# Sparse attention in a two-layer trunk: a third PSUM bank for scores and transposes, gate multiplications on GpSimd, first scores issued between the tiles of memory attention

## The chip, the cores and the metric

The kernel runs on one core of one Trainium2 chip. The metric is the device time of one execution in microseconds (us); the time of a kernel is the median of its runs. Everything is fp32 data. The engines are called as in the profile: PE (TensorE, matrix multiplications and transposes), DVE (VectorE), ACT (ScalarE), POOL (GpSimd), SP (SyncE, which issues most DMA transfers here).

## What is computed

The reference is a trunk of two layers over a sequence of 512 tokens of width 1024. Layer 0 is gated linear attention; layer 1, with which this case deals, is sparse attention with 12 heads of width 64 in 4 groups. Both layers add an attention to a memory of 256 tokens (4 heads), an output projection, and a feed-forward block with a short convolution. The part around the change, cut down:

```python
def nsa_mixer(q, gates, shared, rel_bias):
    kc, vc, ks, vs, kw, vw = shared              # compressed, selected and window keys and values, 4 groups
    ...
        s_c = jnp.einsum('bgrqd,bgkd->bgrqk', qb, kc) + common_bias(d_c)    # 31 compressed keys
        p_c = masked_softmax(s_c, d_c >= 0)
        o_c = jnp.einsum('bgrqk,bgkd->bgrqd', p_c, vc)
        ...
        s_s = jnp.einsum('bgrqd,bgqkd->bgrqk', qb, k_sel) + group_bias(d_s) # selected blocks
        p_s = masked_softmax(s_s, (d_s >= 0)[:, :, None])
        ...
        s_w = jnp.einsum('bgrqd,bgkd->bgrqk', qb, kwb) + common_bias(d_w)   # window
        p_w = masked_softmax(s_w, mask_w)
        ...
        o = gb[..., 0:1] * o_c + gb[..., 1:2] * o_s + gb[..., 2:3] * o_w    # one gate a head and branch
```

16 blocks may be selected and there are only 8, and the window is as long as the sequence, so the selected branch and the window branch are both plain causal attentions over all keys, with keys and values of their own. The gates are sigmoids, one for each token, head and branch.

## The kernel before

**Products.** Most large matrix products are made of three: weights and activations are split into a high and a low part (`wget` for weights: a load of 512 KB, where a gain belongs to it a multiplication on POOL, line 232; the high part `wh` on ACT, line 235; the low part `wl = wraw - wh` on DVE, line 236. `split_to` for activations: high on ACT, line 249, low on DVE, line 250), and high x high, high x low and low x high are accumulated in one bank.

**PSUM.** The eight banks are four pairs, with the tags `acc`, `sc`, `pt` and `po`; asking for a tag gives the next free one of its pair.

**The stage of the change** is the loop over six pairs of heads, `a` = 0 to 5 (heads a and a+6, called hh 0 and 1), in `nsa_layer`. Each pair is done in two steps `s`: first query tiles 0 and 3 (128 and 512 keys), then tiles 1 and 2 (256 and 384 keys), so 12 steps. Generators make the pieces:

- `project(a)`: queries of one pair, 24 matmuls of 512 columns in one `acc` bank, evicted by DVE (line 961, `qf`).
- `queries(a)`: copies of the queries by DMA (`dup`), a strip of bias values from DRAM (line 974), and the split in `Qh` (ACT, line 249) and `Ql` (DVE, line 250).
- `compressed(a)`, in three parts. First: the 31 compressed keys in 8 small products, with `kcT`; both evictions with the bias (DVE, line 1037); minimum and subtraction (DVE, 1040 and 1041; all scores are negated, hence a minimum); exponential (ACT, 1042). Second: mask of the first tile (`cmask`, DVE, 1044), sum and reciprocal (DVE, 1046 to 1048), times the gate (DVE, 1050), and `Pc` times that (DVE, 1051, 128x256). Third: four transposes of `Pc` into a `pt` bank (PE, 947), copied out by ACT (1056).
- `scores(s)`, in six parts, three for each head: a pair of matmuls (K with Qh, K with Ql) into an `sc` bank. For the short tile of a step both branches go into one bank; for the long tile each branch has a bank, so there are the short one, then branch 0, then branch 1. Each is evicted by DVE (line 1078: adds the bias, writes `P` to SBUF and keeps the minimum `smn`) and goes through the exponential on ACT (1080), which also sums (`ssm`). After a head's last part: reciprocal of the sums (DVE, 1082), times the gates (DVE, 1085, 128x4), and then POOL multiplies both `P` tiles of that head by them (1088).
- `weights_t(s)`, in six parts: PE transposes `P` (line 947) into a `pt` bank, and ACT or DVE copies it out (1105, `PT`).
- `values(s)`: PE multiplies `PT` by V and `PcT` by the compressed values (`vcz`) into a `po` bank, one bank for a pair of heads over its two steps.

**What sets the order.** On PE the order of this stage is written by hand: `pe()` chains every matmul and transpose (`mm`, `tr`, lines 946 and 947) to the one before it. In each step there are six rounds; a round issues one part of `scores(s+1)`, one part of `weights_t(s)`, two matmuls of `project(a+2)` (while there is one), and, at fixed rounds, parts of `compressed`, `queries` and `values(s-1)`. The projections of the pairs 0 and 1 come earlier, between the tiles of the memory attention (`mem_att` calls `upto`, which runs the generator `others`). On DVE, ACT, POOL and SP a scheduler sets the order from the order of the program and its own costs; each engine then works in that order.

Of the kernel before, what the change touches and what calls it, by code (L numbers as in the profile page):

```python
# [14 lines left out]
AF = mybir.ActivationFunctionType  # L15
ALU = mybir.AluOpType
# [155 lines left out]
class Trunk:  # L172
# [638 lines left out]
    def nsa_layer(self):  # L811
        nc, I, tc = self.nc, self.I, self.tc
        rc, rb = self.rms_finish(S, "")
        GKV, GMIX = 6, 1
        with ExitStack() as outer:
            pool = outer.enter_context(tc.tile_pool(name="nsa", bufs=1))
            mo = [tuple(self.t(pool, [128, S], f"mo{m}{c}", FR) for c in "hl") for m in range(2)]
            K = [self.t(pool, [128, 2, S], f"K{g}", FR) for g in range(4)]
# [9 lines left out]
            with tc.tile_pool(name="nsap", bufs=2) as pp:  # L828
                T = [self.t(pp, [128, 4, S], f"T{j}", bufs=1) for j in range(2)]
                for j in range(2):  # L830
                    for m in range(2):
# [4 lines left out]
                        for hh in range(2):  # L836
                            g = 2 * m + hh
# [142 lines left out]

            run = lambda g, n=1: [next(g, None) for _ in range(n)]

            with ExitStack() as ms:
                mk = ms.enter_context(tc.tile_pool(name="memk1", bufs=1, side="right"))
                mK, mV = self.mem_kv(1, mk)
                mp = ms.enter_context(tc.tile_pool(name="mema1", bufs=1, side="right"))
# [8 lines left out]
                def others():  # L995

                    gen = project(0)
                    for _ in range(8):
                        yield run(gen, 3)
                    q = queries(0)  # L1000
                    run(q)
                    for i, _ in enumerate(values()):
                        if i == 16:
                            run(q, 3)
                        yield
                    gen = project(1)
                    for _ in range(8):
                        yield run(gen, 3)
# [8 lines left out]
            with tc.tile_pool(name="nsac", bufs=2) as cp:  # L1017
# [4 lines left out]
                def compressed(a):  # L1022
# [3 lines left out]
                    pcs = [self.ps("sc") for _ in range(2)]  # L1026
# [17 lines left out]
                    nc.vector.tensor_tensor(out=Pv[:, 6:8, :], in0=Pv[:, 6:8, :], in1=cmask.unsqueeze(1).to_broadcast([128, 2, 32]), op=ALU.mult)  # L1044
# [5 lines left out]
                    nc.vector.tensor_tensor(out=f.rearrange("p (n b) -> p n b", n=4), in0=f.rearrange("p (n b) -> p n b", n=4), in1=g, op=ALU.mult)  # L1050
                    nc.vector.tensor_tensor(out=Pv, in0=Pv, in1=f.unsqueeze(2).to_broadcast([128, 8, 32]), op=ALU.mult)
# [6 lines left out]

                def scores(s):


                    a, qts = steps[s]
                    for hh in range(2):
                        g = (a + 6 * hh) // 3
                        Q, st = Qs[a][hh], strips[a][hh]
                        f = self.t(self.small, [128, 2, 2], "ssm", bufs=6)
                        for j, qt in enumerate(qts):
                            n = 128 * (qt + 1)
                            ts = slice(128 * qt, 128 * qt + 128)
                            P = Ps[a, qt, hh] = self.t(cp, [128, 2, n], f"P{qt}")  # L1070
                            bias = bass.AP(tensor=st.tensor, offset=st.offset + 383 + n, ap=[st.ap[0], [-1, n]])
                            mn = self.t(self.small, [128, 2], "smn", bufs=6)
                            for brs in ((0, 1),) if qt < 2 else ((0,), (1,)):
                                sc = self.ps("sc")
                                for i in range(2):
                                    mm(sc[:, :n * len(brs)], Q[i][:, ts], K[g][:, brs[0]:brs[-1] + 1, :n], start=i == 0, stop=i == 1)
                                for br in brs:
                                    nc.vector.tensor_tensor_reduce(out=P[:, br, :n], in0=sc[:, n * (br - brs[0]):n * (br - brs[0]) + n], in1=bias, scale=1.0, scalar=3e38,
                                                                   op0=ALU.add, op1=ALU.min, accum_out=mn[:, br:br + 1])
                                    nc.scalar.activation(P[:, br, :n], P[:, br, :n], AF.Exp, scale=-1.0, bias=mn[:, br:br + 1], accum_out=f[:, j, br:br + 1])  # L1080
                                if qt == qts[1] and brs[-1]:
                                    nc.vector.reciprocal(f, f)
                                    gt = bass.AP(tensor=gates.tensor, offset=gates.offset + 36 * qts[0] + 18 * hh + 3 * a + 1,
                                                 ap=[gates.ap[0], [36 * (qts[1] - qts[0]), 2], [1, 2]])
                                    nc.vector.tensor_tensor(out=f, in0=f, in1=gt, op=ALU.mult)  # L1085
                                    for i, t in enumerate(qts):
                                        P = Ps[a, t, hh]
                                        nc.gpsimd.tensor_tensor(out=P, in0=P, in1=f[:, i, :].unsqueeze(2).to_broadcast([128, 2, 128 * t + 128]), op=ALU.mult)  # L1088
                                yield

                def weights_t(s):

                    a, qts = steps[s]
                    for hh in range(2):
                        for qt in qts:
# [3 lines left out]
                            for brs in ((0, 1),) if qt < 2 else ((0,), (1,)):  # L1099
                                pt = self.ps("pt")  # L1100
# [34 lines left out]
                first = scores(0)  # L1135
                for i in range(6):
                    run(first)
                    if i in (1, 3):
                        run(c)
                for s, (a, qts) in enumerate(steps):  # L1140
# [7 lines left out]
                    for i in range(6):  # L1148
# [12 lines left out]
                        if a and qts[0] == 0 and i in (0, 1):  # L1161
                            run(c)
# [32 lines left out]
```

## Time and profile before

| what | value |
|---|---|
| runs | 1338.71, 1340.07 and 1347.0 us, median 1340.07 us |
| the profiled execution | 1337.29 us on the device, its span on the core 1335.5 us |
| PE busy | 1299.7 us, 97% of the span |
| DVE, ACT, POOL busy | 831.7, 591.1 and 119.8 us |
| mean granted TensorE clock | 0.993 of full |
| the stage of the change | from about 769 us (end of memory attention) to about 924 us (output projection) |

A row of the timeline reads: start and duration in us, engine, line, operation, tile written <- tiles read, shape, and count where alike neighbours were put together; in square brackets how long the engine had been idle before, and what ended that. A row of the windows has a stretch of time, its length, busy time and count of each engine, the granted clock of PE, and the share and rate of DMA. In the views of groups, mean durations are in ns.

### The profile page before, as it was taken

How to read it: one execution, taken by the hardware profiler on the slowest of the kernel's cores; microseconds unless marked ns; L12 is line 12 of the kernel's file. 1: busy time of each engine (PE TensorE's matmuls, PEld its weight loads, DVE VectorE, ACT ScalarE, POOL GpSimd, SP SyncE). 2: the span in 40 equal slices, each digit the busy share in tenths (PEclk: the TensorE clock that was granted, in tenths of full speed). 3: DMA queues.
4: the chain of work that ended last, by engine and by line, in shares of the span. 5: the costliest groups of instructions: out<-in, count | busy, mean ns of one | idle time of the engine just before them, and what ended most of it. 6: DMA issues, size and time to landing. Idle time of an engine off the chain costs nothing. (4 is left out here: it accounts for less than half of the span.)

```text
span 1335.5 us, 18101 instructions
## 1 busy us (share of the span) xinstructions
PE 1299.7 (97%) x6934; PEld 1058.8 (79%) x6934; DVE 831.7 (62%) x1372; ACT 591.1 (44%) x1063; POOL 119.8 (9%) x100
## 2 busy tenths in 40 slices
PE   9999998999999999999999988999999999999997
PEld 6887776878888888888788766778878888888886
DVE  7656777567777775334556677675577777773232
ACT  7446554444444443223224565665444444443221
POOL 1000000000000000002114253342000000000000
PEclk9999998999999999999999989999999999999999
DMA  7342110323333333333567223211333333333321
GB/s 249 103 128 78 32 48 17 114 82 100 100 99 95 95 95 95 98 104 111 139 179 227 78 72 93 73 47 32 96 94 96 95 95 95 96 101 102 96 79 63
DMA packets 43002, 129.96 MB, mean 97 GB/s; under 512 B 5719, under 2 KB 9975, under 8 KB 42916
## 3 DMA queue, kind: packets, MB, share of 16 engines
q1 hardware_dynamic: 41504, 126.96, 32.0%
q10 hardware_dynamic: 1412, 1.85, 0.5%
q8 instruction: 55, 0.90, 0.3%
q14 instruction: 31, 0.25, 0.1%
HBM read 116.16 MB, written 2.15 MB: 89 GB/s over the span
## 5 line engine op out<-in xcount | busy, mean ns | idle before, releaser
L236 DVE TENSOR_TENSOR wl<-wraw,wh 128x1024 fp32r<-128x1024 f32 x196 | 245.6, 1253 | 165.3 <-ACT wh L235 163.1
L235 ACT ACTIVATE wh<-wraw 128x1024 fp32r<-128x1024 f32 x196 | 207.5, 1060 | 275.5 <-PE acc L741 92.5
L267 PE MATMUL acc<-xh,wh 128*128 128x512 f32 x800 | 312.9, 391 | 0.0
L267 PE MATMUL acc<-xl,wh 128*128 128x512 f32 x800 | 312.0, 390 | 0.0
L267 PE MATMUL acc<-xh,wl 128*128 128x512 f32 x800 | 310.5, 390 | 0.0
L267 PEld LDWEIGHTS acc<-xh,wh 128*128 128x128 f32 x800 | 150.2, 188 | 32.8 <-issue 1.3
L267 PEld LDWEIGHTS acc<-xl,wh 128*128 128x128 f32 x800 | 150.2, 188 | 31.6 <-issue 0.2
L267 PEld LDWEIGHTS acc<-xh,wl 128*128 128x128 f32 x800 | 150.2, 188 | 31.5 <-issue 0.5
L741 PE MATMUL acc<-ah,wl 128*128 128x512 f32 x352 | 137.0, 389 | 0.0
L741 PE MATMUL acc<-ah,wh 128*128 128x512 f32 x352 | 137.0, 389 | 0.0
L741 PE MATMUL acc<-al,wh 128*128 128x512 f32 x352 | 137.0, 389 | 0.0
L722 DVE TENSOR_TENSOR u<-acc,rb 128x512 f32<-128x512 f32 x88 | 60.6, 688 | 71.2 <-PE acc L267 69.8
L249 ACT ACTIVATE ah<-hc 128x512 fp32r<-128x512 f32 x44 | 27.8, 632 | 116.0 <-DVE hc L729 116.0
L232 POOL TENSOR_TENSOR wraw<-wraw,vec 128x1024 f32<-128x1024 f32 x20 | 38.7, 1942 | 434.6 <-DMA wraw<-in_wp 410.7
L741 PEld LDWEIGHTS acc<-ah,wl 128*128 128x128 f32 x352 | 66.1, 188 | 13.8
L741 PEld LDWEIGHTS acc<-ah,wh 128*128 128x128 f32 x352 | 66.1, 188 | 13.8
L741 PEld LDWEIGHTS acc<-al,wh 128*128 128x128 f32 x352 | 66.1, 188 | 13.5
L724 ACT ACTIVATE hc<-u,vec 128x512 f32<-128x512 f32 x88 | 71.1, 807 | 2.4 <-DVE u L722 1.6
L1088 POOL TENSOR_TENSOR P<-P,ssm 128x256 f32<-128x256 f32 (+3 forms) x48 | 62.4, 1321 | 79.0 <-DVE ssm L1085 43.2
L725 DVE SCALAR_TENSOR_TENSOR hc<-u,vec,hc 128x511 f32<-128x511 f32 x88 | 65.6, 745 | 5.2 <-ACT hc L724 5.2
L726 DVE SCALAR_TENSOR_TENSOR hc<-u,vec,hc 128x510 f32<-128x510 f32 x88 | 66.0, 750 | 3.1
L728 ACT ACTIVATE hc<-hc 128x512 f32<-128x512 f32 x44 | 27.8, 633 | 83.1 <-DVE hc L726 83.1
(334 smaller groups left out, 2050.8 us busy)
## 6 DMA issues: line engine op xcount, KB each, us to landing
wraw<-in_wp SPq DMA_DIRECT2D x200, 512.0 KB, 3.7
strip<-vecd SPq DMA_DIRECT2D x12, 448.0 KB, 3.9
qd<-qf SPq DMA_DIRECT2D x40, 128.0 KB, 2.4
mt<-in_memT SPq DMA_DIRECT2D x16, 128.0 KB, 2.9
kd<-kf SPq DMA_DIRECT2D x16, 128.0 KB, 2.4
out<-wraw SPq DMA_DIRECT2D x3, 512.0 KB, 3.3
h<-in_xT SPq DMA_DIRECT2D x4, 256.0 KB, 6.7
h<-in_xT ACTq DMA_DIRECT2D x4, 256.0 KB, 6.9
```

The source lines that it names most:

```text
L232: nc.gpsimd.tensor_tensor(out=v, in0=v, in1=g, op=ALU.mult)
L235: nc.scalar.activation(wh, raw, AF.Copy)
L236: nc.vector.tensor_tensor(out=wl, in0=raw, in1=wh.bitcast(F32), op=ALU.subtract)
L249: nc.scalar.activation(hi, src, AF.Copy)
L267: self.nc.tensor.matmul(ps[:M, :N], u[:, M * k:M * k + M], x[k][i][:, :N], start=n == 0, stop=n == 23)
L722: nc.vector.tensor_tensor(out=u, in0=ps, in1=rb, op=ALU.mult)
L724: nc.scalar.activation(c, u, AF.Identity, scale=tap(2), bias=tap(3))
L725: nc.vector.scalar_tensor_tensor(out=c[:, 1:], in0=u[:, :S - 1], scalar=tap(1), in1=c[:, 1:], op0=ALU.mult, op1=ALU.add)
L726: nc.vector.scalar_tensor_tensor(out=c[:, 2:], in0=u[:, :S - 2], scalar=tap(0), in1=c[:, 2:], op0=ALU.mult, op1=ALU.add)
L728: nc.scalar.activation(hc[0], hc[0], AF.Silu)
L741: nc.tensor.matmul(ps, a[:, o], x, start=n == 0, stop=n == 3 * NJ - 1)
L1088: nc.gpsimd.tensor_tensor(out=P, in0=P, in1=f[:, i, :].unsqueeze(2).to_broadcast([128, 2, 128 * t + 128]), op=ALU.mult)
```

## The change

Four things are changed, all in `nsa_layer`.

1. **A third bank.** Scores of branch 1 of a long tile go to a `po` bank instead of `sc`; the compressed scores use one `po` and one `sc` bank instead of two `sc`. In the steps 0 to 7 (while there are projections, the last of which frees its `acc` bank in step 7) the transposes of branch 1 of a long tile go to an `acc` bank instead of `pt`.
2. **Gates on GpSimd.** Four of the lines move from DVE to POOL: the mask of `Pc`, the gates on `cf`, `Pc` times `cf`, and the gates on `ssm`. That is 6 + 6 + 6 + 24 = 42 instructions; the count of PE's instructions stays as it was.
3. **The first scores earlier.** `scores(0)` is no longer made after the memory attention, but its six parts go between the groups of three matmuls of `project(1)`, which lie between tiles of the memory attention. The `P` tiles therefore come from a pool (`nsaw`) opened before, two of each as before.
4. **The order of compressed.** Its second part comes in round 0 of the first step of a pair, as before, and its third (the transposes of `Pc`) in round 5 instead of round 1, now for pair 0 too.

The diff, cut (what stands in `scores` and is not shown is the same as before):

```diff
+            def scores(s):
                 a, qts = steps[s]
...
-                            P = Ps[a, qt, hh] = self.t(cp, [128, 2, n], f"P{qt}")
+                        P = Ps[a, qt, hh] = self.t(wp, [128, 2, n], f"P{qt}", bufs=2)
...
-                                sc = self.ps("sc")
+                            sc = self.ps("po" if brs == (1,) else "sc")
...
-                                    nc.vector.tensor_tensor(out=f, in0=f, in1=gt, op=ALU.mult)
+                                nc.gpsimd.tensor_tensor(out=f, in0=f, in1=gt, op=ALU.mult)
...
                 mK, mV = self.mem_kv(1, mk)
+                wp = outer.enter_context(tc.tile_pool(name="nsaw", bufs=1))
...
-                    gen = project(1)
-                    for _ in range(8):
+                    gen, first = project(1), scores(0)
+                    for i in range(8):
+                        if i in (0, 1, 2, 4, 5, 6):
+                            run(first)
                         yield run(gen, 3)
...
-                    pcs = [self.ps("sc") for _ in range(2)]
+                    pcs = [self.ps(tag) for tag in ("po", "sc")]
...
-                    nc.vector.tensor_tensor(out=Pv[:, 6:8, :], in0=Pv[:, 6:8, :], in1=cmask...
+                    nc.gpsimd.tensor_tensor(out=Pv[:, 6:8, :], in0=Pv[:, 6:8, :], in1=cmask...
...
-                    nc.vector.tensor_tensor(out=f.rearrange(...), in0=f.rearrange(...), in1=g, op=ALU.mult)
-                    nc.vector.tensor_tensor(out=Pv, in0=Pv, in1=f.unsqueeze(2)..., op=ALU.mult)
+                    nc.gpsimd.tensor_tensor(out=f.rearrange(...), in0=f.rearrange(...), in1=g, op=ALU.mult)
+                    nc.gpsimd.tensor_tensor(out=Pv, in0=Pv, in1=f.unsqueeze(2)..., op=ALU.mult)
...
-                                pt = self.ps("pt")
+                                pt = self.ps("acc" if brs == (1,) and s < 8 else "pt")
...
-                first = scores(0)
-                for i in range(6):
-                    run(first)
-                    if i in (1, 3):
-                        run(c)
...
-                        if a and qts[0] == 0 and i in (0, 1):
+                        if qts[0] == 0 and i in (0, 5):
                             run(c)
```

How this moves instructions, at three places. (The numbers in the names are those of tiles; the same number is the same tile.)

**First place, PE around the end of the memory attention.** `L946` is `mm`, `L947` is `tr`; `acc<-xh,wh` is the projection of pair 1, `K,Qh` and `K,Ql` are scores of pair 0, `kcT,qf` compressed scores. Before, after the memory attention and the last two of the compressed products:

```order
L946 MATMUL sc_6431<-kcT_5193,qf_6025 128x31
L946 MATMUL sc_6432<-kcT_5193,qf_6025 128x31
L946 MATMUL sc_6452<-K_952_5188,Qh_1173_6215 128x256
L946 MATMUL sc_6452<-K_952_5188,Ql_1174_6216 128x256
L946 MATMUL sc_6461<-K_952_5188,Qh_1173_6215 128x512
L946 MATMUL sc_6461<-K_952_5188,Ql_1174_6216 128x512
L946 MATMUL sc_6473<-K_952_5188,Qh_1173_6215 128x512
L946 MATMUL sc_6473<-K_952_5188,Ql_1174_6216 128x512
L946 MATMUL sc_6485<-K_954_5190,Qh_1176_6221 128x256
L946 MATMUL sc_6485<-K_954_5190,Ql_1177_6222 128x256
L947 MATMUL pt_6492<-ident_101,Pc_6441 64x128 x4
L946 MATMUL sc_6500<-K_954_5190,Qh_1176_6221 128x512
```

Now, within the projection of pair 1, ahead of the last products of the memory attention:

```order
L946 MATMUL sc_6430<-K_954_5190,Qh_1176_6224 128x256
L946 MATMUL sc_6430<-K_954_5190,Ql_1177_6225 128x256
L946 MATMUL acc_6390<-xh_4889,wh_6386 128x512
L946 MATMUL acc_6390<-xh_4889,wl_6387 128x512
L946 MATMUL acc_6390<-xl_4890,wh_6386 128x512
L946 MATMUL sc_6442<-K_954_5190,Qh_1176_6224 128x512
L946 MATMUL sc_6442<-K_954_5190,Ql_1177_6225 128x512
L946 MATMUL acc_6390<-xh_4982,wh_6386 128x512
L946 MATMUL acc_6390<-xh_4982,wl_6387 128x512
L946 MATMUL acc_6390<-xl_4983,wh_6386 128x512
L946 MATMUL po_6450<-K_954_5190,Qh_1176_6224 128x512
L946 MATMUL po_6450<-K_954_5190,Ql_1177_6225 128x512
```

The six score pairs of step 0 stood alone behind the compressed products, with the transposes of `Pc` among them; now three projection matmuls stand between any two of them, and the compressed products come behind them all.

**Second place, PE in the second half of step 0.** `ident,P` are transposes of weights. Before:

```order
L946 MATMUL sc_6605<-K_954_5190,Qh_1176_6221 128x384
L946 MATMUL sc_6605<-K_954_5190,Ql_1177_6222 128x384
L947 MATMUL pt_6611<-ident_101,P_1237_6498 128x128 x4
L946 MATMUL acc_6544<-xl_4710,wh_6540 128x512
L946 MATMUL acc_6544<-xh_4796,wh_6540 128x512
L946 MATMUL sc_6619<-K_954_5190,Qh_1176_6221 128x384
L946 MATMUL sc_6619<-K_954_5190,Ql_1177_6222 128x384
L947 MATMUL pt_6628<-ident_101,P_1237_6498 128x128 x4
L946 MATMUL acc_6544<-xh_4796,wl_6541 128x512
L946 MATMUL acc_6544<-xl_4797,wh_6540 128x512
L946 MATMUL sc_6639<-K_952_5188,Qh_1267_6597 128x256
```

Now:

```order
L946 MATMUL sc_6602<-K_954_5190,Qh_1176_6224 128x384
L946 MATMUL sc_6602<-K_954_5190,Ql_1177_6225 128x384
L947 MATMUL pt_6608<-ident_101,P_1224_6440 128x128 x4
L946 MATMUL acc_6534<-xl_4710,wh_6530 128x512
L946 MATMUL acc_6534<-xh_4796,wh_6530 128x512
L946 MATMUL po_6616<-K_954_5190,Qh_1176_6224 128x384
L946 MATMUL po_6616<-K_954_5190,Ql_1177_6225 128x384
L947 MATMUL acc_6625<-ident_101,P_1224_6440 128x128 x4
L946 MATMUL acc_6534<-xh_4796,wl_6531 128x512
L946 MATMUL acc_6534<-xl_4797,wh_6530 128x512
L947 MATMUL pt_6633<-ident_101,Pc_6496 64x128 x4
L946 MATMUL sc_6642<-K_952_5188,Qh_1266_6594 128x256
```

The second branch's scores and transposes have the tags `po` and `acc`, and the transposes of `Pc` now close the step, ahead of the first scores of step 2.

**Third place, DVE and POOL where the compressed weights of a pair meet its scores.** DVE before, for pair 1, from the last score eviction of a step to the first of the next (`ISA` is line 1078's eviction, `ssm` the sums, `cf` the factors of the compressed part):

```order
L1044 TENSOR_TENSOR Pc_6726<-Pc_6726,cmask_5199 128x64
L961 SCALAR_TENSOR_TENSOR qf_6765<-acc_6544,rb_5175 128x512
L1046 TENSOR_REDUCE cf_6819<-Pc_6726 128x8
L1082 RECIPROCAL ssm_6697<-ssm_6697 128x4
L1047 TENSOR_SCALAR cf_6819<-cf_6819 128x8
L1085 TENSOR_TENSOR ssm_6697<-ssm_6697,gates_5198 128x4
L1048 RECIPROCAL cf_6819<-cf_6819 128x8
L1050 TENSOR_TENSOR cf_6819<-cf_6819,gates_5198 128x8
L1051 TENSOR_TENSOR Pc_6726<-Pc_6726,cf_6819 128x256
L236 TENSOR_TENSOR wl_7430<-wraw_7426,wh_7429 128x1024
L1078 ISA P_1315_6794,smn_6795<-sc_6796,strip_6520 128x256
```

DVE now:

```order
L1081 TENSOR_REDUCE cf_6822<-Pc_6729 128x8
L961 SCALAR_TENSOR_TENSOR qf_6768<-acc_6534,rb_5175 128x512
L1004 RECIPROCAL ssm_6700<-ssm_6700 128x4
L1082 TENSOR_SCALAR cf_6822<-cf_6822 128x8
L1083 RECIPROCAL cf_6822<-cf_6822 128x8
L236 TENSOR_TENSOR wl_7433<-wraw_7429,wh_7432 128x1024
L1000 ISA P_1315_6797,smn_6798<-sc_6799,strip_6510 128x256
```

POOL now, for pair 0 in step 0 (before, there stood only the multiplications of `P` and the memsets):

```order
L1068 MEMSET Pc_6496 128x8
L1079 TENSOR_TENSOR Pc_6496<-Pc_6496,cmask_5199 128x64
L1007 TENSOR_TENSOR ssm_6512<-ssm_6512,gates_5198 128x4
L1010 TENSOR_TENSOR P_1243_6513<-P_1243_6513,ssm_6512 128x512
L1085 TENSOR_TENSOR cf_6538<-cf_6538,gates_5198 128x8
L1010 TENSOR_TENSOR P_1253_6544<-P_1253_6544,ssm_6512 128x768
L1086 TENSOR_TENSOR Pc_6496<-Pc_6496,cf_6538 128x256
```

The four multiplications have left DVE's queue, where `wl` now follows the reciprocal; in POOL's queue `Pc` times `cf` stands behind both multiplications of `P` of a head.

More of the change, by code (lines that the diff above doesn't have):

```diff
@@ L979, in queries @@
                     yield
+            def scores(s):
+                a, qts = steps[s]
+                for hh in range(2):
+                    g = (a + 6 * hh) // 3
+                    Q, st = Qs[a][hh], strips[a][hh]
+                    f = self.t(self.small, [128, 2, 2], "ssm", bufs=6)
+                    for j, qt in enumerate(qts):
+                        n = 128 * (qt + 1)
+                        ts = slice(128 * qt, 128 * qt + 128)
+                        P = Ps[a, qt, hh] = self.t(wp, [128, 2, n], f"P{qt}", bufs=2)
+                        bias = bass.AP(tensor=st.tensor, offset=st.offset + 383 + n, ap=[st.ap[0], [-1, n]])
+                        mn = self.t(self.small, [128, 2], "smn", bufs=6)
+                        for brs in ((0, 1),) if qt < 2 else ((0,), (1,)):
+                            sc = self.ps("po" if brs == (1,) else "sc")
+                            for i in range(2):
+                                mm(sc[:, :n * len(brs)], Q[i][:, ts], K[g][:, brs[0]:brs[-1] + 1, :n], start=i == 0, stop=i == 1)
+                            for br in brs:
+                                nc.vector.tensor_tensor_reduce(out=P[:, br, :n], in0=sc[:, n * (br - brs[0]):n * (br - brs[0]) + n], in1=bias, scale=1.0, scalar=3e38,
+                                                               op0=ALU.add, op1=ALU.min, accum_out=mn[:, br:br + 1])
+                                nc.scalar.activation(P[:, br, :n], P[:, br, :n], AF.Exp, scale=-1.0, bias=mn[:, br:br + 1], accum_out=f[:, j, br:br + 1])
+                            if qt == qts[1] and brs[-1]:
+                                nc.vector.reciprocal(f, f)
+                                gt = bass.AP(tensor=gates.tensor, offset=gates.offset + 36 * qts[0] + 18 * hh + 3 * a + 1,
+                                             ap=[gates.ap[0], [36 * (qts[1] - qts[0]), 2], [1, 2]])
+                                nc.gpsimd.tensor_tensor(out=f, in0=f, in1=gt, op=ALU.mult)
+                                for i, t in enumerate(qts):
+                                    P = Ps[a, t, hh]
+                                    nc.gpsimd.tensor_tensor(out=P, in0=P, in1=f[:, i, :].unsqueeze(2).to_broadcast([128, 2, 128 * t + 128]), op=ALU.mult)
+                            yield
             run = lambda g, n=1: [next(g, None) for _ in range(n)]
```

32 lines of the change are left out of this document (3 added, 29 removed).

## Prediction

> **What bounds the kernel now.** I read the page first (busy time, then the chain that ended last), then the windows of the stage of the change, then PE's gaps in it, and last what DVE and POOL did ahead of each gap.
>
> ```profile
> PE 1299.7 (97%) x6934; PEld 1058.8 (79%) x6934; DVE 831.7 (62%) x1372; ACT 591.1 (44%) x1063; POOL 119.8 (9%) x100
> issue 27%; PE 15%; DVE 2%; ACT 1%; DMA 1%; POOLq 0%; POOL 0%; SPq 0%; DVEq 0%; ACTq 0%
> ```
>
> PE is busy nearly throughout and the change takes no instruction from it, so all it can bring is idle time of PE and time at a lowered clock. The windows tell how much of both lies in the stage:
>
> ```profile
> 769.00:778.00 9.00, 5.40 (x31) 3.66 (x30) 6.84 (x27) 4.42 (x15) 2.73 (x5) 0.71 0.45 117
> 778.00:791.00 13.00, 13.00 (x74) 10.36 (x74) 10.80 (x38) 10.75 (x33) 8.84 (x8) 0.94 0.21 72
> 791.00:817.00 26.00, 23.43 (x204) 18.62 (x200) 19.05 (x60) 16.72 (x49) 10.55 (x10) 1.00 0.29 77
> 817.00:843.00 26.00, 23.20 (x205) 18.60 (x204) 18.55 (x59) 15.83 (x47) 10.29 (x9) 1.00 0.28 77
> 843.00:870.00 27.00, 24.66 (x202) 19.58 (x201) 18.42 (x58) 15.27 (x45) 10.29 (x9) 0.94 0.24 74
> 870.00:896.00 26.00, 24.05 (x209) 18.75 (x209) 20.19 (x63) 17.15 (x49) 11.27 (x9) 1.00 0.22 59
> 896.00:924.00 28.00, 27.18 (x296) 22.75 (x295) 16.09 (x54) 14.93 (x43) 10.04 (x8) 1.00 0.01 3
> ```
>
> Length less the first busy column is PE's idle time: 3.60, 0, 2.57, 2.80, 2.34, 1.95 and 0.82 us, 14.1 in all. The third column from the right is the granted clock. In the first two windows it costs 9 x 0.29 + 13 x 0.06 = 3.4 us, of which about 1 fell on time in which PE was idle anyway, so 2.4; in the fifth, 27 x 0.06 = 1.6. **The ceiling of the change is 14.1 + 2.4 + 1.6 = 18.1 us.** Where the gaps are and what ended them:
>
> ```profile
> 770.73 0.38 PE L946 MATMUL sc<-K,Qh 128*128 128x256 f32 x1 [0.45 <-DVE Pc L1037]
> 772.29 0.47 PE L946 MATMUL sc<-K,Qh 128*128 128x512 f32 x1 [1.06 <-DVE Pc L1037]
> 776.77 1.03 PE L947 MATMUL pt<-ident,Pc 128*64 128x128 f32 x4 [2.10 <-ACT P L1080]
> 794.46 0.51 PE L946 MATMUL sc<-K,Qh 128*128 128x512 f32 x1 [0.26 <-DVE Pc L1037]
> 803.47 0.45 PE L946 MATMUL sc<-K,Qh 128*128 128x384 f32 x1 [1.07 <-DVE smn L1078]
> 805.32 0.66 PE L947 MATMUL pt<-ident,P 128*128 128x128 f32 x4 [1.23 <-ACT PT L1105]
> 856.03 0.44 PE L946 MATMUL sc<-K,Qh 128*128 128x384 f32 x1 [1.12 <-DVE smn L1078]
> 857.88 0.92 PE L947 MATMUL pt<-ident,P 128*128 128x128 f32 x4 [0.77 <-ACT PT L1105]
> 883.90 0.45 PE L946 MATMUL sc<-K,Qh 128*128 128x384 f32 x1 [1.14 <-DVE smn L1078]
> 908.20 0.66 PE L947 MATMUL pt<-ident,P 128*128 128x128 f32 x4 [0.75 <-ACT PT L1105]
> ```
>
> The first three are the boundary, where scores and compressed scores stand alone and share two banks. The pair at 803 and 805 comes back in each pair of heads (856 and 858 are two pairs later): PE waits first for an `sc` bank, then for a `pt` bank. DVE and POOL ahead of that pair of gaps, with two rows for comparison:
>
> ```profile
> 776.14 0.42 DVE L1051 TENSOR_TENSOR Pc<-Pc,cf 128x256 f32<-128x256 f32 x1
> 798.85 2.46 POOL L1088 TENSOR_TENSOR P<-P,ssm 128x256 f32<-128x256 f32 x2 [3.71 <-DVE cf L1048]
> 799.53 2.07 DVE L1051 TENSOR_TENSOR Pc<-Pc,cf 128x256 f32<-128x256 f32 x1
> 801.52 1.21 DVE L236 TENSOR_TENSOR wl<-wraw,wh 128x1024 fp32r<-128x1024 f32 x1
> 802.66 0.41 DVE L1078 CUSTOM_DVE_ANT_0 P<-sc,strip 128x256 f32<-128x256 f32 x1
> 803.34 0.55 DVE L1078 CUSTOM_DVE_ANT_0 P<-sc,strip 128x384 f32<-128x384 f32 x1
> 608.02 1.90 POOL L232 TENSOR_TENSOR wraw<-wraw,vec 128x1024 f32<-128x1024 f32 x1 [333.38 <-DMA wraw<-in_wp]
> 608.25 2.75 DVE L236 TENSOR_TENSOR wl<-wraw,wh 128x1024 fp32r<-128x1024 f32 x1 [4.22 <-ACT wh L235]
> ```
>
> `Pc` times `cf` takes 0.42 us while POOL is idle, and 2.07 when it meets a multiplication of POOL, ending as POOL's ends (801.3). `wl` does the same at 608: 2.75 instead of 1.21. DVE and POOL exclude each other there, for an instruction at a time. Behind the blocked `Pc` stands `wl`, behind that the score evictions; PE's bank comes free at 803.4, and its wait of 1.07 ends.
>
> **The change, part by part.** POOL's durations come from its groups:
>
> ```profile
> L1088 POOL TENSOR_TENSOR P<-P,ssm 128x1024 f32<-128x1024 f32 x12 | 22.9, 1908 | 0.0
> L1088 POOL TENSOR_TENSOR P<-P,ssm 128x768 f32<-128x768 f32 x12 | 18.5, 1539 | 0.0
> L1088 POOL TENSOR_TENSOR P<-P,ssm 128x512 f32<-128x512 f32 x12 | 14.6, 1217 | 36.6 <-DVE ssm L1085 34.2 <-ACT Qh L249 1.9 <-ACT P L1080 0.5
> L1088 POOL TENSOR_TENSOR P<-P,ssm 128x256 f32<-128x256 f32 x12 | 7.4, 618 | 42.5 <-DVE cf L1048 16.4 <-PE sc L946 9.3 <-DVE ssm L1085 9.0
> L1033 POOL MEMSET Pc<- 128x8 f32 x6 | 0.7, 113 | 4.6 <-PE pt L947 4.6
> 634.18 1.17 POOL L307 TENSOR_TENSOR rc<-rc,mhalf 128x4 f32<-128x4 f32 x1 [2.00 <-DVE rc L306]
> ```
>
> So `Pc` times `cf` costs 0.62 us on POOL. The mask (128x64) and the two kinds of gate (128x8, 128x4) have no row there: the memset gives a lower bound of 0.11, the power on 128x4 an upper one of 1.17. I take 0.2, nearer to the memset, since a power is more work than a product. That adds about 0.62 + 6 x 0.2 = 1.8 us a pair of heads to POOL's 10.3 to 11.3 of 26: load is no issue, only place in the queue.
>
> *Boundary, +2.2 us.* The six first score pairs need the same PE time beside `project(1)` as alone, and their evictions have eight groups of projection as cover; idle 3.60 and clock 2.4, 6.0 us, are taken away. Three things come back. First, a pair may still wait for its `sc` bank behind a reduction and a copy of the memory attention on DVE: 0.2 to 0.7, I take 0.45. Second, POOL now multiplies `P` of step 0 (1.91 for the tile of 1024) just as `wl` for `project(2)` comes up on DVE; as at 608 `wl` loses about 1.5, and the eviction of `qf`, the last split of the memory attention and the compressed evictions queue behind it, while PE, past `kcT`, has only one `sc` bank left before it needs an evicted one: 0.9 to 2.2, I take 1.65. Third, `compressed(0)` begins only now, and its transposes stand at the end of step 0. That step lasted 7.5 us, from its first score to the next step's:
>
> ```profile
> 779.45 0.58 PE L946 MATMUL sc<-K,Qh 128*128 128x512 f32 x1
> 787.00 0.28 PE L946 MATMUL sc<-K,Qh 128*128 128x256 f32 x1
> ```
>
> The factor of the first `P` product is there after about half of it and an eviction and exponential, some 5 us in; then POOL's order is `P` of 512 (1.22), `cf` (0.2), `P` of 768 (1.54), `Pc` (0.62): 8.6 us, and PE is at the transposes by about 7. I take 1.7; 0.5 if the factor comes earlier, 3 if the split of `Ql` locks POOL out between two of them. 6.0 - 0.45 - 1.65 - 1.7 = 2.2; from both ends 0.1 to 4.4.
>
> *Steady pairs, 791 to 870, +9.0.* Idle 2.57 + 2.80 + 2.34 and clock 1.6, 9.3 us. The `Pc` multiplication leaves DVE, and `wl` becomes the one that meets POOL's products: it gets in when one of them ends, so DVE is at the evictions by 1 to 2 us sooner than 802.66, in the worst case no sooner. Even then the wait of 1.07 goes, since the second score of 384 takes the `po` bank, whose last reader was done long before; and the 1.23 behind it goes, since those transposes take `acc`. Late next is then the 256 pair of the other head, which needs the bank that the eviction at 803.34 frees at 803.9, with PE there some 2.3 us earlier than before, around 803.6: 0.3 left a pair of heads in that worst case, 0.3 in all in the likely one. The compressed scores lose their waits (0.26 and its like) through the `po` bank. The transposes of `Pc` are in round 5: a pair takes 26.3 us (half the way from 803.47 to 856.03), a step half of that, so round 5 begins some 10 us into it, while POOL's products end about 4 us in (801.3 and `Pc`'s 0.62 and `cf`'s 0.2 behind it). That is 6 us of cover, and at 1.17 for each of POOL's small ones it still holds.
>
> *Tail, 870 to 924, +0.3.* From step 8 on all transposes are on two `pt` banks and no projection fills a round. Of 1.95 + 0.82 = 2.8 I keep 2.5, range 2 to 4.
>
> *Clock, -0.8.* Gaps of 0.45 and 1.06 at the boundary, and 1.12 and 0.77 at 856 to 858, were followed by a lowered clock; the 1.07 and 1.23 at 803 to 805 were not. My new gaps of 1.65 and 1.7 are of that size; such a phase cost 1.6 and 2.4. At two chances in five: 0.8.
>
> The Trainium skill, "TensorE: Matmul & The Clock Gate" (Part 1: The HAM clock gate), has the clock halved only behind a whole idle window of about 3.4 us that runs freely; by it none of these gaps would do, and the sum would be 0.8 better. The rows above, with gaps of 2 us in sum ahead of a granted 0.94, disagree.
>
> **Sum:** 2.2 + 9.0 + 0.3 - 0.8 = 10.7 us. The profiled execution took 1337.29 us around its span of 1335.5, so its span would be 1324.8; it lay 2.8 under the median of the runs, and I subtract from the median: 1340.07 - 10.7 = **1329.4 us**.
>
> **Rivals.**
>
> *Nearly all comes back.* The boundary's two new waits don't arise: POOL's product and `wl` miss each other, and `cf` comes before the `P` products are ready. For it: POOL is idle for most of that stretch (2.73 of 9 us busy). Against it: the order on POOL puts `Pc` behind both products. 6.0 - 0.45 + 9.0 + 0.3 = 14.9, up to the ceiling of 18.1: 1322 to 1325.
>
> *The lock only moves.* `wl` (1.21) and the split of `Ql` each lose as much to POOL's products as `Pc` did (1.65 each), now with longer runs on POOL, so the evictions stay late, and half of the steady gain goes: 2.2 - 1.7 + 4.5 = 5: 1335. For it: 608. Against it: the third bank covers about one round (2.3 us).
>
> *Slower: POOL's queue becomes what PE waits for.* If a small product costs 1.2 us like the power, `cf` and `Pc` come behind two `P` products and up to four of them; where `Pc` then misses its round by 2.5 us in each of six pairs, that is 15 us, and two lowered clocks of 2 us: 1329.4 + 19 = 1348. It outweighs the gain from 1.8 us a pair on. For it: nothing in the trace shows a product that small on POOL. Against it: the 6 us of cover in all pairs but the first.
>
> The Trainium skill, "GPSIMD Engine Reference" (4.1 Engine selection), would keep such elementwise work on VectorE, as GpSimd takes about twice as long with two inputs. Here it is 0.62 against 0.42; by its ratio `Pc` would take 0.84, and the sum be 0.2 worse.
>
> **How the numbers follow.** Forecast 0.50 (1325 to 1333, from the ends of its terms), nearly all 0.28, lock moved 0.16, slower 0.06. A measurement of this kernel tells about 1%, 13.4 us, from no change. Faster by more needs under 1326.7: 0.26 of the first rival and 0.08 of the forecast's lower end, 0.34. Slower by over 1%: 0.05. The rest, 0.61, is within. For 8 in 10 the range runs from the ceiling (1322) to the moved lock and a little over: 1322 to 1336.
>
> **What would show it.** Right: no gap at `sc` behind 770, no granted 0.71 there; a gap of about 1.7 ahead of the first transposes of `Pc`, ended by POOL; `wl` at 2 us or more where POOL multiplies; no gap of the 803 and 805 kind in the pairs 1 to 3. Wrong: gaps ahead of the transposes of `Pc` in every pair (slower rival), the 384 pairs still waiting (moved lock), or a boundary without gaps (first rival).

## The result, and the profile after

| | runs | median us | profiled execution us | its span us | its mean clock |
|---|---|---|---|---|---|
| before | 6 | 1343.24 | 1337.29 | 1335.5 | 0.993 |
| changed | 6 | 1321.87 | 1320.43 | 1318.6 | 0.996 |

The ratio is 0.984, its 95% interval 0.9817 to 0.9863: faster by 1.6%, about 21 us. The forecast was 1329.4 with a range from 1322; its first rival, in which nearly all comes back, named 1322 to 1325. The forecast was taken off 1340.07, the median of three runs; six runs have 1343.24. Between the two profiled executions lie 16.9 us of span; where the 4.5 us beyond that come from is argued below, with the clock.

The windows of the stage in the changed kernel, cut as those of before (length, then busy time of PE, PEld, DVE, ACT, POOL, then granted clock, DMA share, GB/s):

```profile
769.00:778.00 9.00, 8.33 (x54) 5.59 (x52) 6.25 (x19) 5.20 (x13) 6.21 (x7) 1.00 0.38 97
778.00:791.00 13.00, 11.45 (x87) 9.21 (x86) 9.70 (x34) 10.22 (x33) 8.88 (x13) 1.00 0.27 86
791.00:817.00 26.00, 26.00 (x228) 21.13 (x228) 18.33 (x59) 17.97 (x51) 14.10 (x18) 1.00 0.26 77
817.00:843.00 26.00, 26.00 (x246) 21.55 (x245) 18.21 (x57) 18.09 (x51) 14.66 (x20) 1.00 0.30 82
843.00:870.00 27.00, 27.00 (x247) 22.35 (x245) 19.05 (x66) 19.64 (x58) 15.93 (x20) 1.00 0.41 108
870.00:896.00 26.00, 24.99 (x241) 20.20 (x239) 18.37 (x62) 20.38 (x61) 17.93 (x22) 1.00 0.06 20
896.00:924.00 28.00, 28.00 (x202) 23.55 (x201) 12.13 (x17) 9.87 (x15) 0.00 (x0) 1.00 0.19 57
```

PE's idle time is 0.67, 1.55 and 1.01 us in three windows and nothing in the others, 3.2 us instead of 14.1, and the clock is full in all of them. The gaps of 0.2 us and more that are left from 760 to 924, as PE's timeline has them:

```profile
763.42 0.47 PE L946 MATMUL sc<-K,Qh 128*128 128x512 f32 x1 [0.26 <-DVE smn L1000]
775.88 0.41 PE L946 MATMUL sc<-K,Qh 128*128 128x384 f32 x1 [0.67 <-DVE Pc L1072]
783.84 0.62 PE L947 MATMUL pt<-ident,Pc 128*64 128x128 f32 x4 [1.55 <-POOL Pc L1086]
892.47 0.60 PE L947 MATMUL pt<-ident,Pc 128*64 128x128 f32 x4 [0.67 <-ACT PT L1108]
```

The first three are the boundary's new waits, each where the prediction has one (0.45, 1.65 and 1.7 there). The pair of gaps at 803 and 805 has no successor. For the steady part, the first of the compressed products of pair 1 and of pair 4 serve as marks. Before:

```profile
792.89 1.30 PE L946 MATMUL sc<-kcT,qf 64*128 64x31 f32 x16
873.30 1.08 PE L946 MATMUL sc<-kcT,qf 64*128 64x31 f32 x16
```

Changed:

```profile
790.19 0.29 PE L946 MATMUL po<-kcT,qf 64*128 64x31 f32 x1
858.91 0.29 PE L946 MATMUL po<-kcT,qf 64*128 64x31 f32 x1
```

Up to the first mark 2.7 us are won (792.89 - 790.19), of which 0.4 lie ahead of the second head of the memory attention (it begins at 728.72 and 728.36), up to which the two kernels are alike; between the marks, three pairs of heads, 80.41 - 68.72 = 11.7; behind the second (1335.5 - 873.30 against 1318.6 - 858.91) 2.5. The sum is the 16.9 of the spans. What POOL's new instructions take, in its groups of 791 to 870 us:

```profile
L1007 POOL TENSOR_TENSOR ssm<-ssm,gates 128x4 f32<-128x4 f32 x14 | 2.8, 202 | 21.1 <-DVE ssm L1004 15.3 <-DVE cf L1082 4.9 <-PE sc L946 1.0
L1086 POOL TENSOR_TENSOR Pc<-Pc,cf 128x256 f32<-128x256 f32 x4 | 2.5, 616 | 0.3
L1079 POOL TENSOR_TENSOR Pc<-Pc,cmask 128x64 f32<-128x64 f32 x4 | 1.3, 324 | 8.2 <-ACT Pc L1077 8.2
L1085 POOL TENSOR_TENSOR cf<-cf,gates 128x8 f32<-128x8 f32 x4 | 0.8, 204 | 0.0
```

The estimate of 0.2 us for the small ones and 0.62 for `Pc` times `cf` holds (0.20, 0.32 for the mask, 0.62), and POOL in its turn does not hold PE up in these pairs.

### The profile page after: what moved, and what is told of

It is laid out like the page before. It is cut to its first block, busy times and chain, and to the rows that moved or that the text cites. A ratio compares the mean times of both kernels' runs of the same rounds, so it can differ in the third digit from the quotient of the medians.

```text
span 1318.6 us, 18055 instructions
## 1 busy us (share of the span) xinstructions
PE 1293.0 (98%) x6934; PEld 1056.9 (80%) x6934; DVE 815.5 (62%) x1330; ACT 591.6 (45%) x1063; POOL 136.8 (10%) x142
## 3 DMA queue, kind: packets, MB, share of 16 engines
HBM read 116.16 MB, written 2.15 MB: 90 GB/s over the span
## 5 line engine op out<-in xcount | busy, mean ns | idle before, releaser
L1010 POOL TENSOR_TENSOR P<-P,ssm 128x256 f32<-128x256 f32 (+3 forms) x48 | 65.5, 1384 | 1.9
```

## The experiments

In all, `e1` to `e4` take parts of the change alone, `e5` to `e8` take parts away from it, and `e9` to `e12` follow what was left. `e1` to `e4`, `e5` to `e8` and `e9` to `e12` each ran beside runs of the kernel before of their own, with medians of 1342.78, 1340.85 and 1343.2 us; the changed kernel has 1343.24 beside it. A difference of medians between two of these sets is therefore sure to some 2 to 3 us only. "Pair" is the time between the first compressed products of the pairs 1 and 2, "clock" the granted clock in the window 769 to 791 (in late executions, `e2`, `e5` and `e8`, up to 3 us of this part of the program lie beyond it), "gap" PE's idle time ahead of the second head of the memory attention at about 728 us, up to which the kernels of `e1` to `e9` are alike.

| kernel | median us | ratio to before, 95% interval | span us | pair us | clock | gap us |
|---|---|---|---|---|---|---|
| before | 1343.24 | 1 | 1335.5 | 26.26 | 0.84 | 1.50 |
| e1 bank alone | 1330.05 | 0.9905, 0.9887 to 0.9924 | 1326.5 | 23.15 | 0.84 | 3.14 |
| e2 gates (and order) alone | 1328.19 | 0.9888, 0.9865 to 0.991 | 1330.4 | 23.43 | 0.84 | 4.12 |
| e3 order alone | 1338.0 | 0.9959, 0.9938 to 0.998 | 1334.4 | 25.19 | 0.77 | 2.15 |
| e4 first scores (and order) alone | 1334.42 | 0.9928, 0.9908 to 0.9948 | 1333.9 | 25.24 | 0.92 | 3.20 |
| e5 without bank | 1326.24 | 0.9884, 0.986 to 0.9907 | 1325.9 | 23.49 | 0.92 | 2.05 |
| e6 without gates | 1321.85 | 0.9861, 0.9837 to 0.9886 | 1320.2 | 22.89 | 1.00 | 1.71 |
| e7 without first scores | 1327.35 | 0.9896, 0.9876 to 0.9916 | 1324.0 | 22.89 | 0.84 | 2.85 |
| e8 `Pc` of pair 0 on DVE | 1321.32 | 0.9856, 0.9834 to 0.9878 | 1323.2 | 22.90 | 1.00 | 4.55 |
| changed | 1321.87 | 0.984, 0.9817 to 0.9863 | 1318.6 | 22.90 | 1.00 | 0.97 |
| e9 `Pc` of pair 0 later | 1318.46 | 0.982, 0.9796 to 0.9845 | 1316.8 | 22.92 | 1.00 | 1.23 |

The last column warns of comparing single spans: one and the same part of the program costs 1.0 to 4.6 us, with the execution. Spans are compared below only from a mark behind it, or by medians.

**The third bank alone (e1).** On the kernel before:

```diff
-pcs = [self.ps("sc") for _ in range(2)]
+pcs = [self.ps(tag) for tag in ("po", "sc")]
-sc = self.ps("sc")
+sc = self.ps("po" if brs == (1,) else "sc")
-pt = self.ps("pt")
+pt = self.ps("acc" if brs == (1,) and s < 8 else "pt")
```

Expected: 

> The kernel before with the third bank alone (scores of the second branch and one of the compressed on po, transposes of the second branch on acc in steps 0 to 7); gates on DVE, first scores alone behind the memory attention, order of compressed as before. Theory BANK (PE waited for banks; a third one lets it run past DVE's lateness, whatever made DVE late): the waits of 1.07 and 1.23 and those of the compressed scores go, about 3 us a pair in the steady pairs, span 10 to 14 us under 1335.5, though Pc times cf still takes 2.07 us under POOL. Theory LOCK (the lateness itself, Pc times cf held up by POOL, has to leave DVE): only the compressed waits and part of the boundary go, 2 to 4 us, and a gap of about 1 us stays ahead of the 384 scores.

DVE is as late as before, and PE no longer minds. DVE's rows ahead of the place where the two gaps were:

```profile
801.66 2.07 DVE L1051 TENSOR_TENSOR Pc<-Pc,cf 128x256 f32<-128x256 f32 x1
803.66 1.21 DVE L236 TENSOR_TENSOR wl<-wraw,wh 128x1024 fp32r<-128x1024 f32 x1
804.79 0.41 DVE L1078 CUSTOM_DVE_ANT_0 P<-sc,strip 128x256 f32<-128x256 f32 x1
```

And the windows of the boundary and of the steady pairs of this kernel:

```profile
769.00:791.00 22.00, 16.75 (x92) 13.06 (x89) 16.25 (x61) 14.52 (x45) 9.03 (x11) 0.84 0.30 91
791.00:870.00 79.00, 79.00 (x706) 63.51 (x706) 62.93 (x202) 54.33 (x158) 36.44 (x31) 1.00 0.27 76
```

The multiplication takes its 2.07 us, and still PE is busy for 79.00 of 79.00. It is 12.7 us by medians and 9.0 by spans, with 1.6 us more in the gap at 728: theory BANK. The boundary is no better (5.25 us idle, clock 0.84).

**The gates alone (e2), with the transposes of `Pc` in round 5.** On the kernel before, `nc.vector` becomes `nc.gpsimd` in the four lines of the change, and:

```diff
-if a and qts[0] == 0 and i in (0, 1):
+if a and qts[0] == 0 and i in (0, 5):
```

Expected: 

> The kernel before with the four multiplications on POOL alone, and the transposes of Pc in round 5 (in round 1 they would come before POOL is done); banks and first scores as before. BANK: DVE gets to its evictions up to 2 us sooner, but wl takes the place of Pc under POOL's product, so half of the 1.07 and 1.23 stays: 3 to 5 us under 1335.5. LOCK: 8 us or more under it, and no gap ahead of the 384 scores.

This is what LOCK said: 14.6 us by medians (5.1 by spans, with 2.6 us more in the gap at 728), and no gap ahead of the 384 scores in the steady pairs. Two banks are enough as soon as DVE is on time; the windows of this kernel's steady pairs, and the row of `wl` there:

```profile
791.00:870.00 79.00, 77.62 (x678) 63.49 (x676) 54.59 (x178) 55.53 (x163) 46.04 (x57) 1.00 0.30 86
```

```profile
L236 DVE TENSOR_TENSOR wl<-wraw,wh 128x1024 fp32r<-128x1024 f32 x3 | 4.6, 1530 | 0.7 <-ACT wh L235 0.7
```

`wl` does meet POOL, but takes 1.53 us instead of 1.21: it loses 0.3, where `Pc` lost 1.65. So both theories hold, each by itself: the bank hides DVE's lateness, the gates (with the order, see e3) remove it, and neither needs the other.

**The order alone (e3).** The diff shown for e2, without the gates. Expected: 

> The kernel before with the transposes of Pc in round 5 instead of round 1 for the pairs 1 to 5, nothing else. Both theories: within 1.5 us of 1335.5; the one gap of 0.76 that PE had there in pair 4 goes. This is the part of e2 that is not the gates.

The pair falls from 26.26 to 25.19 us, which neither theory had. With the transposes of `Pc` out of round 1 the `pt` bank is free there, and the gap of 1.23 is gone; the other one grew from 1.07:

```profile
804.67 0.42 PE L946 MATMUL sc<-K,Qh 128*128 128x384 f32 x1 [1.49 <-DVE smn L1078]
```

DVE is still late there: in the next two pairs by `Pc` times `cf` as before (2.07 us each, with gaps of 1.66 and 1.64), and in this pair by `wl`. `Pc` times `cf` took 0.73 us, and `wl` behind it lost to POOL's products in its place:

```profile
800.92 2.91 DVE L236 TENSOR_TENSOR wl<-wraw,wh 128x1024 fp32r<-128x1024 f32 x1
```

Of the 2.83 us that e2 brings a pair (26.26 to 23.43), 1.07 may thus be the order's. It has a price, too: from the first compressed product of pair 4 to the end, e3 and e4 take 464.5 and 464.6 us against 462.2 before, with a granted clock of 0.93 from 870 to 896.

**The first scores alone (e4), with the order.** The changed kernel with `sc` and `pt` for all tags as before and the four lines back on `nc.vector`. Expected: 

> The kernel before with the first scores between the groups of project(1), and the order of compressed that this needs (third part in round 5, pair 0 too); all gates on DVE, two sc banks. Both theories: kcT comes 3.5 us later than before and step 1 begins 2 to 4 us sooner than 787.0, no lowered clock at 769 to 778; the steady pairs stay at 26.3 us each. Span 2 to 4 us under 1335.5. If the boundary's lowered clock was worth more than the 2.4 us that I made of it, 5 or more.

Its pair is 25.24, the order's again. It is 8.4 us by medians (1.6 by spans, with 1.7 us more in the gap at 728); of the 8.4, e3 has 4.8. The boundary is better and not clean: clock 0.92 instead of 0.84 or 0.77, and a gap of 1.78 us ahead of the first 512 scores of step 1, which wait for the compressed eviction on one of two `sc` banks.

**Without the bank (e5).** The changed kernel with the diff of e1 undone. Expected: 

> The changed kernel with two sc and two pt banks as before (no third bank). BANK: the steady pairs go back from 22.9 to 25 us or more each, span 8 to 12 us over 1318.6. LOCK: 3 us over it at most.

Neither fits: by medians 4.4 us over the changed kernel, the pair 23.49 and not 25. In the steady pairs the gates do most of the bank's work. From the gap at 728 on, the profile has the same 4.4 us, in three parts: 1.6 up to the mark of pair 1, where the gap ahead of the scores is 1.77 instead of 0.67 and the clock 0.92; 1.75 in the three steady pairs (70.47 against 68.72); and 1.1 behind them.

**Without the gates (e6).** The changed kernel with the four lines back on `nc.vector`. Expected: 

> The changed kernel with the four multiplications back on DVE (42 instructions). BANK: the third bank covers DVE's lateness, span within 3 us of 1318.6, either way, and the gap of 1.55 ahead of the first transposes of Pc gone, since POOL's queue is out of that chain. LOCK: Pc times cf is at 2.07 again and PE waits in each pair, span 6 to 10 us over 1318.6.

The pair is 22.89, the median 1321.85 against 1321.87, though the group of its multiplication reads as it did before:

```profile
L1086 DVE TENSOR_TENSOR Pc<-Pc,cf 128x256 f32<-128x256 f32 x4 | 8.3, 2070 | 0.1
```

With the bank and the first scores in place, the gates on POOL bring nothing in the steady pairs (68.71 us for three against 68.72) and nothing that the medians can tell. Behind them the profile shows a gain: from the first compressed product of pair 4 to the end this kernel takes 461.5 us, the changed one 459.7. The part of the expectation that missed is the first transposes of `Pc`: the gap is there with the multiplications out of POOL's queue, too:

```profile
783.62 0.60 PE L947 MATMUL pt<-ident,Pc 128*64 128x128 f32 x4 [1.68 <-POOL P L1010]
```

It ends with a product of POOL, for the reason shown under e8: on DVE the gate on `cf` of pair 0 took 1.02 us (0.17 alone) and `Pc` times `cf` 1.28 (0.42 alone).

**Without the first scores (e7).** The changed kernel with `scores(0)` behind the memory attention, as before. Expected: 

> The changed kernel with the first scores behind the memory attention as before. Both theories: steady pairs stay at 22.9 us; step 1 begins later than 784.2, by 1 to 3 us, and the granted clock falls again in 769 to 778. Span 2 to 4 us over 1318.6.

By medians it is 5.5 us over the changed kernel, more than the 2 to 4 expected; from the gap at 728 on, the profile has 2.9. The window 769 to 791 of this kernel, with 4.8 us idle and the lowered clock back:

```profile
769.00:791.00 22.00, 17.20 (x95) 13.04 (x92) 15.46 (x55) 15.08 (x46) 11.05 (x18) 0.84 0.31 91
```

**`Pc` of pair 0 on DVE (e8).**

```diff
-nc.gpsimd.tensor_tensor(out=f.rearrange(...
-nc.gpsimd.tensor_tensor(out=Pv, in0=Pv, ...
+eng = nc.gpsimd if a else nc.vector
+eng.tensor_tensor(out=f.rearrange(...
+eng.tensor_tensor(out=Pv, in0=Pv, ...
```

Expected: 

> The changed kernel with the gate on cf and Pc times cf of pair 0 alone on DVE (two instructions). If POOL's queue is what the first transposes of Pc wait for, the gap of 1.55 us at 783.84 falls to 0.5 or less and the span to 1317.0 to 1317.8. If the chain up to cf is as late, or Pc times cf meets a product of POOL and takes 2 us, the gap stays over 1 us and the span at 1318.6.

The gap stays, at 1.79 us: to take the two multiplications out of POOL's queue does not remove it. PE's row, and DVE's ahead of it:

```profile
788.29 0.60 PE L947 MATMUL pt<-ident,Pc 128*64 128x128 f32 x4 [1.79 <-issue]
784.57 1.35 DVE L250 TENSOR_TENSOR Ql<-qd,Qh 128x512 fp32r<-128x512 f32 x1 [0.16 <-ACT Qh L249]
785.84 1.43 DVE L1086 TENSOR_TENSOR cf<-cf,gates 128x8 f32<-128x8 f32 x1
787.67 0.41 DVE L1087 TENSOR_TENSOR Pc<-Pc,cf 128x256 f32<-128x256 f32 x1
```

The second way of the expectation came about, with `cf` in the place of `Pc`. POOL multiplies two tiles of `P` from 784.33 to 787.24, and `Ql` (0.69 alone) and the gate on `cf` (0.17 alone) lose 1.9 us to it, as much as the gap. In the changed kernel the same two products of POOL stand ahead of `Pc` in POOL's own queue:

```profile
780.13 1.04 POOL L1010 TENSOR_TENSOR P<-P,ssm 128x512 f32<-128x512 f32 x1
781.12 0.65 POOL L1085 TENSOR_TENSOR cf<-cf,gates 128x8 f32<-128x8 f32 x1
781.74 1.46 POOL L1010 TENSOR_TENSOR P<-P,ssm 128x768 f32<-128x768 f32 x1
783.17 0.61 POOL L1086 TENSOR_TENSOR Pc<-Pc,cf 128x256 f32<-128x256 f32 x1
```

So by the rows POOL's products of `P` make the gap on either engine; no run took them out of the way to show it.

**`Pc` of pair 0 later (e9).** On the changed kernel:

```diff
-if qts[0] == 0 and i in (0, 5):
+if qts[0] == 0 and i in ((0, 5) if a else (0,)) or s == 1 and i == 1:
```

Expected: 

> The changed kernel with the transposes of Pc of pair 0 in round 1 of step 1 instead of round 5 of step 0, nothing else. Putting the two products of pair 0 back on DVE left the gap there (1.79 us, against 1.55), so it is not POOL's queue alone but the whole chain of compressed(0), which begins too late whatever engine ends it. Theory CHAIN: with some 2 us more of PE's work ahead of them the transposes wait for nothing, the gap of 1.55 goes, 1.5 us off the span from the first score of pair 0 to that of pair 1. Rival: the values of step 0, right behind, now wait for the copy of PcT instead, and less than 0.5 us is won.

The gap goes, as CHAIN said. That does not tell the chain from POOL's products, since more of PE's work ahead of the transposes covers either. The window of this kernel has 0.67 us idle where the changed one has 2.22:

```profile
769.00:791.00 22.00, 21.33 (x147) 16.19 (x146) 17.50 (x55) 15.88 (x46) 15.92 (x20) 1.00 0.29 91
```

From the second head of the memory attention (728.69 us here, 728.36 there) to the compressed products of pair 1 it takes 59.60 us against 61.83. The median is 1318.46, the lowest of all; by the ratios' intervals it can't be told from the changed kernel, by the gap in the trace it can.

**The strips of pair 0 later (e10), with e9 (e11), and on the kernel before (e12).**

```diff
+ld = nc.sync.dma_start(strip, ...)
+if a == 0:
+    tc.add_manual_dep(ld.ins, d.ins.name, ..., reason="order")
```

Here `d` is the last query copy of the pair. Expected of e10: 

> The changed kernel with the two strip loads of pair 0 (448 KB each) put behind the query copies of that pair in SP's queue; in the profiles so far PE's gap ahead of the second head of the memory attention (at about 728 us, ended by Qh) was between 0.97 and 4.55 us in ten executions of kernels that are alike up to there. Theory LOADS: the strips compete with the copies that this gap waits for; without them it is under 1.2 us, and the time falls 1 to 3 us under the changed kernel's. Rival: the weight loads of 512 KB do that, and gap and time stay as they are.

Of e11: 

> Both: the transposes of Pc of pair 0 in round 1 of step 1, and the strips of pair 0 behind its query copies. By the sum of CHAIN and LOADS 2.5 to 4.5 us under the changed kernel, 1317.5 to 1319.5 as median; if neither holds, 1321 to 1322.

Of e12: 

> The kernel before with the strips of pair 0 behind its query copies, nothing else. Its runs without profile were 4 to 6 us longer than its profiled execution and their mean clock 0.985 to 0.992, against 0.993. If late copies at 728 are what spreads them, its runs come within 3 us of each other and their median 3 us or more under the kernel before; if the lowered clock in the stage of the change spreads them, the spread stays at 6 us or so and the median within 2 us.

The gap at 728 is 0.90, 0.31 and 0.89 us in the three profiles, under 1.2 as LOADS said, and the time does not follow: e10 1321.34 us (ratio 0.9838), e11 1319.52 (0.9822), e12 1342.12 (0.9994, interval 0.9977 to 1.0011). In the changed kernel's own profile that gap was 0.97 to begin with, so there was little to win, and part of it comes back: behind it all three have two gaps that the other profiles don't have, 0.34 us ahead of the next scores, ended by `Ql`, and 0.42 to 0.77 at 736, ended by `Qh`. e11 is 1.1 us over e9, not under it. e12's ten runs, 1339.41 to 1344.82 us at mean clocks of 0.991 to 0.985, still spread over 5.4 us (9.7 in the thirteen runs of the kernel before), and the interval of their ratio holds 1. So the late copies don't account for the spread of before; its lowered clock is the candidate that is left. e12's trace speaks for it: its gaps of 1.08 and 1.24 us at 805 and 807 are followed by a granted 0.93 from 791 to 817, where before has 1.00 behind gaps of 1.07 and 1.23, and its pair takes 27.65 us instead of 26.26. The windows of e12 show the lowered clock again in the stage:

```profile
769.00:791.00 22.00, 18.69 (x97) 14.02 (x94) 16.16 (x62) 14.89 (x47) 9.80 (x11) 0.77 0.28 86
791.00:870.00 79.00, 71.29 (x595) 56.39 (x595) 55.97 (x170) 46.77 (x133) 30.46 (x27) 0.96 0.26 72
```

## Why the prediction was wrong

Where the gaps were, what made them and which would go was right; two sizes and one sign were not, and all three erred to the same side. A fourth term, the boundary, came out near by luck.

- **"Clock, -0.8": this is the step that failed.** It charged the new gaps at the boundary with lowered clocks. Gaps of 0.67 and 1.55 us came, and the clock stayed full. More weighs that one profiled execution was taken for what the clock costs before. The kernel before had a mean clock of 0.985 to 0.992 in the thirteen runs beside `e9` to `e12`, 0.989 on average, against 0.993 in the profile; the run at 0.985 was the longest (1347.3 us), the one at 0.992 the shortest (1337.62). The changed kernel had 0.995 or 0.996 in six. An estimate of the time lost is one less the mean clock, times the time: 0.007 x 1335.5 = 9.3 us in the profile of before and 0.004 x 1318.6 = 5.3 in that of the change, about 4 apart; 0.0109 x 1343 = 14.6 and 0.0047 x 1322 = 6.2 in the runs, about 8 apart. That is some 4 of the 4.5 us by which the medians (21.4) differ by more than the spans (16.9); with the medians of the clocks (0.990 and 0.995) it is 3. The clock is on record to three digits, and for the six runs of before in the result not at all, so more than its size can't be told. In the sum of the prediction, the clock should have stood with some +3 to +4 beyond the 4.0 already in the boundary and the steady part, not with -0.8. By the two profiles alone the sum is 6.2 short: 2.7 in the steady pairs, 2.2 in the tail, 0.8 of the clock and 0.5 at the boundary.
- **"Steady pairs, +9.0": right in mechanism, 2.7 short.** Measured are 11.7. The 9.3 from the windows were taken for a ceiling, and were not one. In a pair without clock loss (26.26 to 22.90, so 3.4 us) the windows have 2.6 to 2.8 idle; the rest is in time that the windows count as busy: the 16 compressed products ahead of the 512 scores, 1.31 us until the next row before and 1.01 now; four pairs of 384 scores, 1.68 and 1.41, where all of the difference lies in the one pair right behind the gap of 1.07 (0.62 instead of 0.35). Whether these are waits too short to be listed or the price of starting again is not shown. And it named the bank as what makes the two gaps go even if DVE is no sooner: e1 shows just that. That the gates would do it alone (e2) it did not say, nor that the order is worth 1.0 us a pair (e3); it costed the new round at nothing.
- **"Boundary, +2.2": 2.7 up to the mark, 2.3 without what lies ahead of 728, with terms that miss each other.** The first stall was 0.26 (0.45 said), the second 0.67 (1.65), the third 1.55 (1.7), 1.3 us less than said. Against that, PE waits for DVE at 741 and 748 for 1.39 and 1.20 us instead of 0.58 and 0.54, 1.5 more, which the sum had not; these two came to 0.4 in e6 and 1.4 in e9, so that how much of them is the change's is open. The second stall was over-sized since `wl` was said to lose to POOL. It won, and POOL lost:

```profile
772.19 1.28 DVE L236 TENSOR_TENSOR wl<-wraw,wh 128x1024 fp32r<-128x1024 f32 x1 [0.77 <-ACT wh L235]
```

```profile
772.35 2.87 POOL L1010 TENSOR_TENSOR P<-P,ssm 128x1024 f32<-128x1024 f32 x1
```

  `wl` began 0.16 us sooner; the product of 1024 elements took 2.87 us instead of 1.9. The third has the size said and, by POOL's rows (under e8), the reason said: 3.65 us from the first product to the end of `Pc`, where the prediction has 3.58, and the split of `Ql` in the way of the gate on `cf`. What the prediction did not have is that DVE is no way out: there the same products of POOL hold the multiplications up (e6, e8). More work ahead of the transposes removes the gap (e9).
- **"Tail, +0.3": 2.5 measured.** It had been given nearly all of its 2.8 us of gaps again; two of 0.18 and 0.67 us and a few smaller ones are left, 1.0 in all. From the first compressed product of pair 4 to the end, before has 462.2 us, the bank alone (e1) 461.9, the gates with the order (e2) 460.8, the change 459.7; without the gates (e6) it is 461.5, without the bank (e5) 460.8. Profiles of kernels that are alike there (the change, e7 to e11) lie within 0.4. So both work there, too, the gates more than the bank, though the transposes have only `pt`.
- **The rivals.** "Nearly all comes back" named the time, not the way: its two waits did arise (0.67 and 1.55). "The lock only moves" fell, for `wl` lost 0.3 in the steady pairs (1.53 us in the change as in e2) and not 1.65; with the order alone (e3) it did move, in one pair of three. "POOL's queue becomes what PE waits for" came in the first pair only, with 0.20 us for the small products in the others.

What remains open: why the clock is lowered after some gaps and not after others. In the window 769 to 791 it was lowered in every profile with the first scores alone behind the memory attention (0.77 or 0.84), less in those with first scores early and two banks (0.92), and in none with first scores early and the third bank. That is an order of cases, with a gap of 1.79 us (e8) on the full side and one of 1.78 (e4) on the lowered one, and no rule. The Trainium skill, "TensorE: Matmul & The Clock Gate" (Part 1: The HAM clock gate), has it lowered after an idle window of about 3.4 us; no gap of the stage here is that long, so that rule alone does not give these drops. Ahead of the stage there are longer ones: the gap at 728 was followed by a granted 0.50 to 0.71 from 731 to 735 where it was 4.55, 4.12, 3.20 or 2.05 us long (e8, e2, e4, e5), and by a full clock where it was 3.14 or 2.85 (e1, e7).

## What to carry to other kernels

Where one engine waits for another's lateness through a buffer, there are two cures, a further buffer and the removal of the lateness, and they don't add: here each brought the pair from 26.3 to about 23.3 us and both together to 22.9, so it pays to test the second one alone before keeping it. Look at what frees a buffer as well as at what fills it: moving four transposes to another round was worth 1.0 us a pair, and by itself cost 2.3 us behind the pairs. And read the mean clock of several runs, not of the profiled one alone, before a gap's price is written down: a gap costs twice where the clock falls behind it, and the same gap does so in one execution and not in another.

## What the runs showed of the hardware

- DVE and POOL exclude each other in either direction, and the one that starts first wins: `wl` 0.16 us ahead of POOL took 1.28 us and POOL's product 2.87 (1.91 alone); `Pc` times `cf` behind POOL took 2.07 (0.42 alone). The Trainium skill, "SBUF — State Buffer" (Who interferes with whom), says that issue order decides who blocks, for instructions of DVE with two inputs in SBUF; the trace agrees.
- A product of 128x4 or 128x8 takes POOL 0.20 us, one of 128x64 0.32 us.
- The idle time in the windows is no ceiling: a pair came out 0.6 to 0.8 us shorter than it says, and rows right behind a gap are longer (384 scores at 803.47 before took 0.45 us, at 798.54 in the changed kernel 0.34).
- The granted clock behind the same gaps differs with the execution: behind gaps of 1.07 and 1.23 us it was 1.00 in before, behind 1.08 and 1.24 it was 0.93 in e12.
